# Depthwise convolution of an encoder layer: how its 31 taps are divided among the engines

## The chip, the cores and the metric

The kernel runs on one core of one Trainium2 chip. The metric is the device time of one execution in microseconds (us). The core has a matrix engine (TensorE, "PE" in the rows; "PEld" is its weight load), a vector engine (VectorE, DVE), a scalar engine (ScalarE, ACT), a general engine (GpSimd, POOL) and a queue engine (SyncE, SP) that issues most of the transfers. Each engine takes its instructions in order from a queue of its own; semaphores tie the queues together.

## The reference

One layer on 1024 tokens of width 1024, in float32. A first sub-layer projects the normalised input and splits the columns in two groups: a convolution module and an RWKV-7 recurrence in chunks; both go through one output projection. A second sub-layer chooses 128 of 16384 one-neuron experts for each token. The part that the change touches is the causal depthwise convolution over 31 taps and 512 channels:

```
u = p_conv[..., :CONV_WIDTH] * jax.nn.sigmoid(p_conv[..., CONV_WIDTH:])
u = lax.conv_general_dilated(u, conv_w[:, None, :], window_strides=(1,),
    padding=[(CONV_KSIZE - 1, 0)], feature_group_count=CONV_WIDTH) + conv_b
y_conv = silu(layer_norm(u, conv_ln_g, conv_ln_b))
```

Every channel has 31 weights of its own, so a tap is one multiplication by a weight per channel and one addition. Channels lie on the 128 partitions (four tiles `ct` of 128), tokens along the free dimension, in two halves of 512.

## The kernel before, in words

Two halves of the sequence, `h` = 0 and 1, are projected by `inproj(h)`: it normalises the tokens, transposes them to channels (`to_channels`, L210), splits them and the weights in two terms, and multiplies each weight tile in 24 matmuls (`proj`, L182). A projected tile leaves PSUM by two ScalarE copies and one VectorE operation (`shifted`, L325 to L329); `mixed` (L384) makes the operands of the recurrence from it, with two multiplications on GpSimd (L409, L421). `cond_some` (L248) reduces rows of the conditioning weights on VectorE in between. `glu` fills `ubuf`, the input of the convolution, and appends the generator `conv(h)` to the list `slow`.

The recurrence runs over 16 chunks: `solve(c)` and `pass_state(c)` are long chains of small matmuls on TensorE (L604, L635, L655, ...) with VectorE and ScalarE steps between them. After every few of their matmuls `fill()` is called: it advances the list `side` (`inproj(1)`, then the output projections `post`) by `RUN` = 4 steps whenever the credit allows, and with every fourth call (`SLOW` = 4) it advances `slow` by one `yield`. So one `yield` of `conv` is the unit in which the convolution is spread over the recurrence. `conv(0)` lies beside the start of the recurrence and `inproj(1)`. `conv(1)` begins when `inproj(1)` has written its last `u` and lies beside `post(0)`, the output projection of the first 256 tokens, which splits its weights with GpSimd (L170). What is left of `conv(1)` is drained at chunk 8 (L975).

`conv(h)` does for each of four channel tiles: one VectorE `tensor_scalar` (tap 0 with the bias, L453), 17 VectorE `scalar_tensor_tensor` (taps 1 to 17, L458, `a = u*w + a`, both `u` and `a` in SBUF), and for taps 18 to 30 a diagonal matrix made by ScalarE (L464, 128 x 128) and a float32 matmul of it with the window of `u` (L466, two matmul records each), summed in PSUM in `pt`. At the end `V.tensor_add(a, a, pt)` (L469) joins the two. Three VectorE taps and two matmul taps make one `yield`: 7 yields for a tile. After the four tiles the layer norm over channels follows (L472 to L484), then the swish (L488 to L491) and the store to `conv_d`.

The pages of the shared pool `pgp` (`NPAGE` = 35 pages of 128 x 512) hold `cacc` (L451), `ctap` (L462) and nearly every other temporary of `inproj`, `conv` and `post`. PSUM tiles `mm` are three (`NMM`); `pt` holds one of them for as long as a tile's taps last.

The order on each engine is not written out by hand: a scheduler of the framework takes, for each engine, the ready instruction that stands earliest in the program, by its own estimate of times, and fixes the order at compile time. On the chip the queues then run in that order, whatever the true durations are.

After the recurrence come the last `post`, the choice of experts (`choose`, `gate_matrix`) and the expert stage (L1156, L1190), which begins at about 1600 us and takes the rest.

Of the kernel before, what the change touches and what calls it, by code (L numbers as in the profile page):

```python
# [15 lines left out]
AF = mybir.ActivationFunctionType  # L16
# [9 lines left out]
KS = 31  # L26
# [53 lines left out]
def layer_kernel(ctx, tc, x, cols, c_row, cond_w, w_in, w2a2, g2, w_out, ln_rows, wq, keys, peer_u, peer_ut, peer_v, peer_vt, out):  # L80
    nc = tc.nc
    V, A, G, T = nc.vector, nc.scalar, nc.gpsimd, nc.tensor
# [10 lines left out]
    def col(n, i=None):  # L93
        a, b = COFF[n]
        return colt[:, a:b] if i is None else colt[:, a + i:a + i + 1]
# [50 lines left out]
    def mm(w=512):  # L146
        return psum.tile([128, 512], F32, tag="mm", name="mm")[:, :w]
# [4 lines left out]
    def page(name, dt=F32, w=512):  # L152
        return pgp.tile([128, max(w, 512)], dt, tag="pg", name=name)[:, :w]
# [117 lines left out]
    def inproj(h, ps, pg_):  # L271
# [60 lines left out]
        def glu():  # L332
            while conv_left:
                slow_step(1)
            for ct in range(4):
                if first and ct == 0:
                    pa, pg = first
                else:
                    pa = yield from tile_of(ct)
                    pg = yield from tile_of(4 + ct)  # L340
                s_ = tp("gsig")
                A.activation(s_, pg, AF.Sigmoid)
                A.activation(ubuf[:, ct, :KS - 1], utail[:, ct, :], AF.Copy)
                V.tensor_mul(ubuf[:, ct, KS - 1:], pa, s_)
                A.activation(utail[:, ct, :], ubuf[:, ct, HALF:], AF.Copy)
                if h == 1:
                    cond_some(range(32 + 4 * ct, 36 + 4 * ct))
            slow.append(conv(h))
            conv_left.append(h)
# [90 lines left out]


    slow, gates, gb, conv_left, psg, tail = [], [], [], [], [], []
    PE_TAPS = 13

    def conv(h):
        acc = []
        for ct in range(4):
            wk = lambda k: colt[:, COFF["conv_w"][0] + KS * ct + k:COFF["conv_w"][0] + KS * ct + k + 1]
            win = lambda k: ubuf[:, ct, k:k + HALF]

            a, pt = page("cacc"), mm()  # L451
            acc.append(a)
            V.tensor_scalar(a, win(0), wk(0), col("conv_b", ct), op0=OP.mult, op1=OP.add)  # L453
            i, j = 1, KS - PE_TAPS
            while i < KS - PE_TAPS or j < KS:
                for _ in range(3):
                    if i < KS - PE_TAPS:
                        V.scalar_tensor_tensor(a, win(i), wk(i), a, op0=OP.mult, op1=OP.add)  # L458
                        i += 1
                if j < KS:  # L460
                    n = min(2, KS - j)
                    dg = page("ctap").rearrange("p (k c) -> p k c", k=4)  # L462
                    for k in range(n):
                        A.activation(dg[:, k, :], ident, AF.Copy, scale=wk(j + k))  # L464
                    for k in range(n):
                        T.matmul(pt, dg[:, k, :], win(j + k), start=j + k == KS - PE_TAPS, stop=j + k == KS - 1)  # L466
                    j += n
                yield
            V.tensor_add(a, a, pt)  # L469
        pmn = mm()  # L470
        for ct in range(4):
            T.matmul(pmn, ones_m, acc[ct], start=ct == 0, stop=ct == 3)  # L472
        for ct in range(4):
            V.tensor_sub(acc[ct], acc[ct], pmn)
        yield
        pv = mm()
        for ct in range(4):
            s2 = page("s2")
            A.activation(s2, acc[ct], AF.Square)
            T.matmul(pv, ones_m, s2, start=ct == 0, stop=ct == 3)  # L480
        rs = page("crs")
        A.activation(rs, pv, AF.Sqrt, bias=eps_ln)
        V.reciprocal(rs, rs)
        yield  # L484
        for ct in range(4):
            y = acc[ct]
            V.tensor_mul(y, y, rs)
            A.activation(y, y, AF.Identity, bias=col("cln_b", ct), scale=col("cln_g", ct))  # L488
            sc_ = page("csig")
            A.activation(sc_, y, AF.Sigmoid)  # L490
            G.tensor_mul(y, y, sc_)  # L491
            ld(conv_d[h][ct], y)
            yield
        conv_left.remove(h)
# [643 lines left out]
    for g in range(32):  # L1138
# [4 lines left out]
        for e in range(4):  # L1143
# [7 lines left out]
            for bs in NBLK:  # L1151
                p = mg(NW)
                i = 0
# [99 lines left out]
```

## Time and profile before

| | us |
|---|---|
| median of 3 runs | 3366.39 (3362.37 to 3373.07) |
| the profiled execution | 3369.74 |
| its span, first to last instruction | 3367.7 |
| mean granted share of TensorE's clock in it | 0.936 |

The rows below come from that one profiled execution. In the rows an instruction stands as engine, line, operation, output and inputs by the program's names. "Busy" is the time in which an engine executes; the chain is the sequence of work that ended last, followed back from the end of the program, each step from what released it or from the instruction before it on its engine. The convolution lies in two stretches, from 215 to 330 us (`conv(0)`) and from 535 to 640 us with a remainder to 720 us (`conv(1)`).

### The profile page before, as it was taken

The page shows a single profiled execution, that of the slowest core. Times are in us where ns is not written, and L with a number is a line of the kernel's source. Part 1 is how long each engine was busy: PE and PEld are TensorE (multiplying, and loading weights), DVE is VectorE, ACT ScalarE, POOL GpSimd, SP SyncE. Part 2 cuts the span into 40 slices and gives each one's busy share as a digit, 9 for nine tenths or more (in the row PEclk, how much of TensorE's full clock was granted, in tenths as well). Part 3 has the DMA queues.
Part 4 walks back from the last instruction along what each step waited for, and adds up shares of the span by engine and source line. Part 5 has one row for each costly group of instructions (what it writes and reads, how often), then busy time and mean ns, then how long its engine had stood idle before and what let it go on. Part 6 is the DMA issues. An engine that isn't in the chain of part 4 may idle for free.

```text
span 3367.7 us, 54601 instructions
## 1 busy us (share of the span) xinstructions
PE 3039.8 (90%) x20400; PEld 2652.4 (79%) x20400; DVE 2523.1 (75%) x5590; ACT 1246.3 (37%) x2479; POOL 1734.8 (52%) x1328
## 2 busy tenths in 40 slices
PE   6969999999888665676999999999999999999996
PEld 5735766678777665675899999999999989998985
DVE  5398567657676697779777778777787877777788
ACT  5552543443545435654322222322222232222222
POOL 2400112234122154313877777787777768777772
PEclk9979999799889777787999999999999999999998
DMA  8875564467556757465999999898999989999994
GB/s 307 292 258 170 163 178 163 155 236 269 168 194 206 250 173 230 141 213 174 360 345 330 348 333 342 323 361 324 356 330 346 327 327 347 349 337 342 332 345 163
DMA packets 398393, 918.09 MB, mean 273 GB/s; under 512 B 77184, under 2 KB 210480, under 8 KB 376112
## 3 DMA queue, kind: packets, MB, share of 16 engines
q1 hardware_dynamic: 205296, 469.96, 39.8%
q0 software_dynamic: 110592, 402.70, 32.4%
q10 hardware_dynamic: 82240, 41.94, 4.4%
q8 instruction: 160, 2.62, 0.3%
q14 instruction: 105, 0.86, 0.1%
HBM read 786.55 MB, written 127.95 MB: 272 GB/s over the span
## 4 chain that ended last, share of the span: by engine, by line
PE 71%; DVE 14%; DMA 8%; ACT 3%; issue 2%; POOL 1%; SPq 0%; DVEq 0%; POOLq 0%; ACTq 0%
PE mg L1156 25%; PE md L1190 25%; PE mm L182 11%; DMA G_d<-stage 5%; PE mgate L958 3%; DVE cacc L458 2%; DVE cw L248 1%; PE bank L635 1%; DVE oa L940 1%; DVE ob L952 1%; PE bank L655 1%; DMA cw<-cond_w 1%; PE mm L828 1%; PE mm L466 1%; PE bank L604 1%
## 5 line engine op out<-in xcount | busy, mean ns | idle before, releaser
L1156 PE MATMUL mg<-h2h,uhi 128*128 128x320 f32 x2048 | 634.0, 310 | 0.0
L1156 PE MATMUL mg<-h2l,uhi 128*128 128x320 f32 x2048 | 633.8, 309 | 0.0
L1156 PE MATMUL mg<-h2h,ulo 128*128 128x320 f32 x2048 | 633.5, 309 | 0.0
L1190 PE MATMUL md<-vhi,ah 128*128 128x512 f32 x1280 | 492.7, 391 | 23.0 <-ACT vhi L1119 16.1
L1190 PE MATMUL md<-vhi,al 128*128 128x512 f32 x1280 | 498.2, 390 | 0.0
L1190 PE MATMUL md<-vlo,ah 128*128 128x512 f32 x1280 | 497.0, 390 | 0.0
L1093 DVE SCALAR_TENSOR_TENSOR gy<-grow,gz,gy 128x1024 f32<-128x1024 f32 x381 | 488.6, 1282 | 6.4 <-DMA grow<-peer_v,eid 2.7
L1086 DVE SCALAR_TENSOR_TENSOR grow<-grow,gh 128x1024 f32<-128x1024 f32 x384 | 458.9, 1213 | 34.8 <-DMA grow<-peer_u,eid 30.9
L1078 POOL DMA_INDIRECT grow<-peer_v,eid x384 | 361.0, 940 | 163.4 <-DVE gy L1093 85.0
L1078 POOL DMA_INDIRECT grow<-peer_u,eid x384 | 361.4, 941 | 159.6 <-issue 70.8
L1156 PEld LDWEIGHTS mg<-h2h,uhi 128*128 128x128 f32 x2048 | 385.8, 188 | 6.0
L1156 PEld LDWEIGHTS mg<-h2l,uhi 128*128 128x128 f32 x2048 | 385.8, 188 | 5.1
L1156 PEld LDWEIGHTS mg<-h2h,ulo 128*128 128x128 f32 x2048 | 385.6, 188 | 3.9
L1119 ACT ACTIVATE vhi<-vraw 128x1024 fp32r<-128x1024 f32 x128 | 135.6, 1062 | 635.4 <-PE md L1190 434.8
L1195 DVE TENSOR_TENSOR yacc<-md,yacc 128x512 f32<-128x512 f32 x310 | 210.6, 688 | 186.5 <-PE md L1190 180.7
L1121 POOL TENSOR_TENSOR vlo<-vraw,vhi 128x1024 fp32r<-128x1024 f32 x128 | 306.3, 2414 | 68.7 <-ACT vhi L1119 62.7
L958 PE MATMUL mgate<-oa,ob 128*128 128x128 f32 x1280 | 213.3, 321 | 141.2 <-ACT stage L959 97.3
L1121 POOL TENSOR_TENSOR ulo<-uraw,uhi 128x1024 fp32r<-128x1024 f32 x128 | 310.9, 2429 | 50.0 <-ACT uhi L1119 43.6
L958 PEld LDWEIGHTS mgate<-oa,ob 128*128 128x128 f32 x1280 | 190.8, 228 | 154.3 <-ACT stage L959 92.2
L1190 PEld LDWEIGHTS md<-vhi,ah 128*128 128x128 f32 x1280 | 240.7, 188 | 70.7 <-ACT vhi L1119 16.4
L1190 PEld LDWEIGHTS md<-vlo,ah 128*128 128x128 f32 x1280 | 240.3, 188 | 48.5
L1190 PEld LDWEIGHTS md<-vhi,al 128*128 128x128 f32 x1280 | 240.3, 188 | 44.0
(347 smaller groups left out, 5837.7 us busy)
## 6 DMA issues: line engine op xcount, KB each, us to landing
uraw<-peer_ut SPq DMA_DIRECT2D x128, 512.0 KB
vraw<-peer_vt SPq DMA_DIRECT2D x128, 512.0 KB
wsplit<-split_wq SPq DMA_DIRECT2D x48, 1024.0 KB
G_d<-stage ACTq DMA_DIRECT2D x20, 2048.0 KB
gmat<-G_d SPq DMA_DIRECT2D x32, 1280.0 KB
cw<-cond_w SPq DMA_DIRECT2D x48, 512.0 KB
wsplit<-split_w_out SPq DMA_DIRECT2D x24, 1024.0 KB
split_w_in<-wsplit SPq DMA_DIRECT2D x22, 1024.0 KB
```

Source lines behind the costliest of these rows:

```text
L182: T.matmul(pt, l[:, k, :], r[k], start=i == 0, stop=i == 3 * KD - 1)
L248: V.scalar_tensor_tensor(w, w, 1.0, silc, op0=OP.mult, op1=OP.mult, accum_out=mod[:, j:j + 1])
L458: V.scalar_tensor_tensor(a, win(i), wk(i), a, op0=OP.mult, op1=OP.add)
L958: T.matmul(pt[:, t, :], ob[:, t, :], oa[:, t, :], start=True, stop=True)
L1078: G.indirect_dma_start(out=r, out_offset=None, in_=peer_u if k < 128 else peer_v, in_offset=bass.IndirectOffsetOnAxis(ap=eid[:, k % 128:k ...
L1086: V.scalar_tensor_tensor(r, r, 1.0, ht, op0=OP.mult, op1=OP.mult, accum_out=z[:, i:i + 1])
L1093: V.scalar_tensor_tensor(y, r, z[:, i - 128:i - 127], y, op0=OP.mult, op1=OP.add)
L1119: A.activation(hi, raw, AF.Copy)
L1121: G.tensor_sub(lo, raw, hi.bitcast(F32))
L1156: T.matmul(p, l[:, k, :], r[k][:, bs], start=i == 0, stop=i == 3 * KD - 1)
L1190: T.matmul(p, l[:, ts], r[:, e % 2, :], start=e == 0 and q == 0, stop=e == 3 and q == 2)
L1195: V.tensor_add(ya, p, ya)
```

## The change

The taps 18 to 30 of TensorE are divided again. Taps 18 to 23 become six ScalarE products (`activation` with Copy and a scale per channel, 128 x 512): the first is written to a new page `cgps` (`b`), the other five to pages `cprod`, each of which GpSimd adds to `b`. Taps 24 to 30 stay on TensorE as diagonal products, seven in place of thirteen. At the end of a tile GpSimd adds `b` to `a`, and then VectorE adds `pt` as before. VectorE keeps the taps 0 to 17. One `yield` now holds four VectorE taps, one product with its addition, and two matmul taps: 5 yields for a tile in place of 7.

```
-    PE_TAPS = 13
+    PE_TAPS, POOL_TAPS = 7, 6
...
-            a, pt = page("cacc"), mm()
+            a, b, pt = page("cacc"), page("cgps"), mm()
...
-            i, j = 1, KS - PE_TAPS
-            while i < KS - PE_TAPS or j < KS:
-                for _ in range(3):
-                    if i < KS - PE_TAPS:
+            n_dve = KS - PE_TAPS - POOL_TAPS
+            A.activation(b, win(n_dve), AF.Copy, scale=wk(n_dve))
+            i, m, j = 1, n_dve + 1, KS - PE_TAPS
+            while i < n_dve or m < KS - PE_TAPS or j < KS:
+                for _ in range(4):
+                    if i < n_dve:
                         V.scalar_tensor_tensor(a, win(i), wk(i), a, op0=OP.mult, op1=OP.add)
                         i += 1
+                if m < KS - PE_TAPS:
+                    p_ = page("cprod")
+                    A.activation(p_, win(m), AF.Copy, scale=wk(m))
+                    G.tensor_add(b, b, p_)
+                    m += 1
                 if j < KS:
...
                 yield
+            G.tensor_add(a, a, b)
             V.tensor_add(a, a, pt)
```

## Rows read from the trace of the kernel before

**Rows 1.** The page: busy time by engine, and the chain by line.

```profile
PE 3039.8 (90%) x20400; PEld 2652.4 (79%) x20400; DVE 2523.1 (75%) x5590; ACT 1246.3 (37%) x2479; POOL 1734.8 (52%) x1328
...
PE mg L1156 25%; PE md L1190 25%; PE mm L182 11%; DMA G_d<-stage 5%; PE mgate L958 3%; DVE cacc L458 2%; DVE cw L248 1%; PE bank L635 1%; DVE oa L940 1%; DVE ob L952 1%; PE bank L655 1%; DMA cw<-cond_w 1%; PE mm L828 1%; PE mm L466 1%; PE bank L604 1%
```

**Rows 2.** Busy time of each engine by stretch; the header names the columns.

```profile
core 0: us, PE busy (x) PEld busy (x) DVE busy (x) ACT busy (x) POOL busy (x), PEclk, DMA share, GB/s
215.00:285.00 70.00, 61.17 (x176) 33.57 (x176) 69.81 (x122) 25.71 (x67) 4.75 (x3) 0.92 0.81 246
285.00:330.00 45.00, 41.22 (x277) 26.79 (x277) 40.55 (x101) 12.81 (x32) 1.50 (x1) 0.89 0.43 136
330.00:440.00 110.00, 109.91 (x1077) 79.79 (x1077) 60.46 (x110) 53.63 (x106) 13.67 (x11) 1.00 0.54 162
535.00:600.00 65.00, 60.74 (x408) 39.18 (x409) 56.89 (x75) 22.68 (x58) 16.23 (x8) 0.95 0.35 124
600.00:640.00 40.00, 37.45 (x368) 27.14 (x367) 30.17 (x59) 13.82 (x31) 9.74 (x5) 0.87 0.54 184
640.00:680.00 40.00, 37.25 (x384) 29.98 (x383) 25.35 (x70) 19.28 (x43) 5.61 (x5) 0.50 0.43 123
```

**Rows 3.** The chain by line within 190 to 330, 535 to 640, 640 to 700 us.

```profile
by line: DVE cacc L458 25.5%; DVE cw L248 21.4%; PE mm L182 6.1%; DVE nr L402 4.7%; DMA cw<-cond_w 4.6%; DMA bv_d<-sq 3.2%; DMA xt<-x 2.9%; PE mm L472 2.7%; DVE hlo L220 2.6%; PE bank L604 1.7%; DVE cum L392 1.6%; DVE sq L417 1.4%; PE mm L4
...
by line: DVE cacc L458 38.1%; issue 14.6%; PE mm L466 13.9%; PE mm L182 11.8%; DMA ycf<-rwkv_d 4.7%; POOL wsplit L170 2.2%; PE bank L635 1.7%; POOL xt L788 1.7%; PE bank L661 1.6%; POOL yclo L762 1.5%; DVE cacc L469 1.2%; DVE MT L658 1.0%; 
...
by line: PE mm L182 15.6%; PE mm L466 10.0%; DMA xt<-x 8.1%; PE mm L216 7.2%; PE bank L693 6.1%; PE mm L472 6.1%; PE bank L691 5.9%; PE bank L635 4.8%; PE bank L655 4.3%; PE bank L604 3.3%; DVE bnst L190 3.2%; PE bank L643 2.4%; PE bank L73
```

**Rows 4.** Single lines: ns least/median/most, first and last start in us.

```profile
L458 DVE SCALAR_TENSOR_TENSOR cacc<-u,colt,cacc x136: 628/747/2908, 218.1 to 634.0; 128x512 f32<-128x512 f32 x136
...
L466 PE MATMUL mm<-u,ctap x208: 590/592/1221, 217.4 to 691.4; 128*128 128x512 f32 x104
...
L464 ACT ACTIVATE ctap<-ident,colt x104: 384/390/414, 214.0 to 681.8; 128x128 f32<-128x128 f32 x104
...
L479 ACT ACTIVATE s<-cacc x8: 629/633/658, 326.4 to 698.9; 128x512 f32<-128x512 f32 x8
...
L491 POOL TENSOR_TENSOR cacc<-cacc,csig x8: 1265/1282/1735, 349.1 to 718.8; 128x512 f32<-128x512 f32 x8
```

**Rows 5.** Timeline, 215 to 264 us: start us, us, engine, line, names, count.

```profile
220.30 4.45 PE L466 MATMUL mm<-u,ctap 128*128 128x512 f32 x10
...
229.41 1.02 PE L419 MATMUL m<-sq,ones_h 128*128 128x512 f32 x2
...
248.29 1.44 POOL L409 TENSOR_TENSOR a<-a,nr 128x512 f32<-128x512 f32 x1 [22.68 <-DVE nr L404]
248.52 1.76 DVE L458 SCALAR_TENSOR_TENSOR cacc<-u,colt,cacc 128x512 f32<-128x512 f32 x1
...
259.29 1.40 DVE L458 SCALAR_TENSOR_TENSOR cacc<-u,colt,cacc 128x512 f32<-128x512 f32 x2
...
261.28 2.41 DVE L458 SCALAR_TENSOR_TENSOR cacc<-u,colt,cacc 128x512 f32<-128x512 f32 x2
261.49 1.66 POOL L421 TENSOR_TENSOR xm<-xm,W 128x512 f32<-128x512 f32 x1 [11.76 <-issue]
```

**Rows 6.** Groups by line, 190:330 (first two) and 535:640: busy us, mean ns.

```profile
L458 DVE SCALAR_TENSOR_TENSOR cacc<-u,colt,cacc 128x512 f32<-128x512 f32 x68 | 51.9, 789 | 0.1
L248 DVE SCALAR_TENSOR_TENSOR cw<-cw,silc 128x1024 f32<-128x1024 f32 x27 | 32.7, 1215 | 1.4 <-DMA cw<-cond_w 1.4
...
L458 DVE SCALAR_TENSOR_TENSOR cacc<-u,colt,cacc 128x512 f32<-128x512 f32 x68 | 62.3, 917 | 1.5
L170 POOL TENSOR_TENSOR wsplit<-wraw,wsplit 128x1024 fp32r<-128x1024 f32 x8 | 20.0, 2504 | 64.4 <-ACT wsplit L169 64.4
```

**Rows 7.** Line 466 alone, 285 to 330 us: PE busy and weight loads.

```profile
285.00:330.00 45.00, 11.43 (x26) 4.83 (x26) 0.89 0.43 136
```

**Rows 8.** Timeline, 676 to 700 us, of ScalarE and of VectorE.

```profile
679.82 1.85 ACT L464 ACTIVATE ctap<-ident,colt 128x128 f32<-128x128 f32 x6
...
692.05 0.69 DVE L469 TENSOR_TENSOR cacc<-cacc,mm 128x512 f32<-128x512 f32 x1 [10.36 <-PE mm L466]
```

## The prediction

> **What bounds the kernel now.** I read the page first. Half of the chain is the expert stage, lines 1156 and 1190 [rows 1], which the change does not touch. The line that the change thins out, 466, is about 1% of the chain; the vector taps of line 458, of which it keeps all, are 2% [rows 1]. So the question is what ends last in the two stretches where the convolution runs, not what is busiest over the span.
>
> The second view is busy time by stretch. From 215 to 285 us VectorE is busy for 69.81 of 70 us, TensorE for 61.17, GpSimd for 4.75; from 285 to 330 VectorE has 40.55 of 45 and TensorE 41.22; from 535 to 600 VectorE has 56.89 of 65 and TensorE 60.74 [rows 2]. Two engines are nearly full, so the table can't tell which is last. The chain does: from 190 to 330 us its first two lines are VectorE's taps (25.5%) and VectorE's reductions of line 248 (21.4%); line 466 stands nowhere in the list, whose last whole entry is 1.4%. From 535 to 640 us the taps of VectorE are 38.1%, which is 40 of 105 us, and line 466 is 13.9%, 14.6 us [rows 3]. Between the two, from 330 to 440 us, TensorE is busy for 109.91 of 110 us [rows 2], but no tap is in it. The reader is to see that VectorE bounds both stretches, with TensorE close behind, and that the change leaves VectorE its taps 0 to 17: 18 before, 18 after. "Divided in three" is a division of TensorE's thirteen.
>
> The third view is the timeline, for what a new GpSimd instruction does to VectorE. Two taps alone take 1.40 us; two taps with a GpSimd multiplication of 1.66 us beside them take 2.41. One tap has a median of 747 ns [rows 4]; with a GpSimd multiplication of 1.44 us beside it one takes 1.76 [rows 5]. Both times VectorE loses 1.0 us. The groups agree: in the second stretch, where line 170 runs on GpSimd for 20.0 us, the same 68 taps take 62.3 us, against 51.9 in the first [rows 6].
>
> **The change part by part.** *Additions on GpSimd.* A tile gets five additions of products and one of `b` to `a`: 6, so 24 in each `conv(h)`, 48 in all. The nearest row for one is line 491, the same shape, median 1.28 us [rows 4]; they are 31 us for each `conv`, and GpSimd has that room in both stretches [rows 2]. The price is VectorE's: 1.0 us for each that meets a tap [rows 5]. It can be nothing, where the addition meets an idle VectorE, and 1.28, where VectorE stands still for all of it; I take 1.0, since the two measured cases are of this very instruction on VectorE and of GpSimd instructions of this shape. How many meet: VectorE is busy for 110.4 of 115 us from 215 to 330, 96%, and line 248, its other large load there, 32.7 us, also reads two tiles of SBUF [rows 2, 6]. That gives 24 x 1.0 x 0.96 = 23 us for `conv(0)`. For `conv(1)` I count three tiles, 18 additions, because the last tile's taps on TensorE come only after ScalarE has made their matrices at 680 us, when VectorE idles for 10.36 us before line 469 [rows 8]; there I read a lack of free pages, and the additions of the last tile, which need pages too, would wait with them. VectorE is busy for 87.1 of 105 us, 83%: 18 x 1.0 x 0.83 = 15 us. Together 38 us of VectorE, all on its queue, in stretches where the chain runs through that queue.
>
> The Trainium skill, "SBUF — State Buffer", section "Who interferes with whom", has a rule that speaks against this change: a VectorE instruction with two SBUF inputs and a GpSimd instruction that reads SBUF exclude each other for the whole instruction. The two cases above agree in kind; by the whole instruction the 42 additions would cost 42 x 1.28, before the shares some 54 us in place of 42, and the sum would be about 10 us higher.
>
> *Matmuls off TensorE.* 6 taps x 8 tiles = 48 taps of two records each. Ten records in a row take 4.45 us, or 0.43 us apart when the last one's 0.59 is taken off [rows 4, 5] (4.45 - 0.59, over 9), so 48 x 2 x 0.43 = 41 us leave TensorE. What of it is on the chain: 14.6 us of line 466 from 535 to 640, 6.0 us from 640 to 700 (10.0% of 60), and under 1.4% of 140 us, 2 us, in the first stretch [rows 3]: some 22 us, of which 6/13 go, 10 us. To that I add the taps from 285 to 330 us, 11.43 us [rows 7], of which 6/13 are 5 us: what TensorE has done by then of the projections shortens the stretch after 330, where it is full. So -15; the bounds are -10 and -41. I stay near the lower one because while VectorE is the later engine a freer TensorE finds nothing ready.
>
> *ScalarE.* 48 diagonal matrices of 390 ns go, 48 products come; the nearest row is line 479, 128 x 512 from SBUF, 633 ns [rows 4]: +11.7 us, under a ScalarE that is busy for 25.71 of 70 us [rows 2]. I count nothing; without that cover it would be the 11.7.
>
> *Waits.* `V.tensor_add(a, a, pt)` now waits for GpSimd's last addition, which waits for the tile's last tap: 1.28 us or more, 8 times, with the next tile's taps and line 248 queued behind it on VectorE. The scheduler can put those in front, so I take 0 of a bound of 10 us. On GpSimd the multiplications of lines 409 and 421, in the first stretch, and the subtraction of line 170, in the second, now queue behind additions, one of which waits for VectorE; a queue fixed at compile time by times that a blocked VectorE does not keep makes them late. TensorE's order shows how freely the scheduler mixes: taps of `conv(0)` stand at 220 us, ahead of line 419 of the earlier `inproj(0)` at 229 [rows 5]. Bound 0 to 10 us, taken 0. `yield`s fall from 7 to 5 for a tile, so the convolution is asked for earlier beside the recurrence; total VectorE work to its end is the same, so I count 0, and no sign is excluded. Five `cprod` and one `cgps` page come for a tile and three `ctap` pages go, which can only lengthen the wait for pages.
>
> The sum on the profiled execution: 3369.7 + 23 + 15 - 15 = 3392.7 us. That execution is 3.3 us over the median of the runs, so on medians 3366.4 + 23 = 3389.4; I say 3389.
>
> **The rivals.** *TensorE was the bound after all (faster).* It is busy for 98.2 of 105 us in the second stretch and for 109.91 of 110 from 330 to 440 [rows 2]. If the additions fall where VectorE waits or works from one tile, and TensorE uses the freed time for projections ahead of the full stretch, -15 to -41 is left: 3325 to 3351, say 3340. It decides from the point where fewer than about 15 of the 42 additions meet a busy VectorE. Against it stands a VectorE with 0.2 us of idle time in 70.
>
> *The two balance.* Half of the additions meet a tap, 19 us, against 15 to 20 of TensorE: 3356 to 3376, say 3366. For it speaks that from 600 to 640 us VectorE has 9.8 us free [rows 2].
>
> *A late queue or a slower clock on top of the forecast.* From 640 to 680 us TensorE runs at a granted share of 0.50, its lower level of 1.2 GHz, and is busy for 37.25 us [rows 2], which at 2.4 GHz would be about 18.6. A TensorE with 41 us less to do idles more beside VectorE; one more stretch like this costs some 18 us, and so do the two queue waits above together at their bounds: 3407. The Trainium skill, "TensorE: Matmul & The Clock Gate", section "What's actually happening", says that "the default state is throttled, and activity releases the throttle", by which removing matmuls has this price; the rows show only that the clock was 0.87 from 600 to 640 us and 0.50 after it, not what it fell for.
>
> **How the numbers follow.** Forecast 0.55, balance 0.18, TensorE as the bound 0.18, late queue or clock 0.09. The predicted time is the forecast's, 3389. Its own range runs from 3377 (-15 becomes -27) to 3412 (all 42 additions at the 1.28 bound, no relief beyond 10 us: 3366 + 54 - 10 = 3410). For 8 in 10 I take in the balance and the start of the faster rival, and above it most of the late queue: 3350 to 3420, which leaves out about 0.16 below and 0.03 above. A difference of 0.3%, 10 us, is about what a measurement of this kernel can tell from no change. Slower by more: 0.55 + 0.09 = 0.64; within: 0.18; faster by more: 0.18.
>
> **What would show it.** Right: line 458 with a mean well over 0.79 us in the first stretch (about 1.1 with some 20 additions in it), taps that end after GpSimd's additions, the first chunk's operands and the end of `conv(0)` some 20 us later, and TensorE with more idle time before 330 us. Wrong: taps still at 0.75 us beside additions (the price); additions in gaps of VectorE (the count); the stretch from 330 us on shortened by as much as the first grew (the relief); a mean clock lower than 0.936 of the span with VectorE unchanged (the clock).

## The result

The changed kernel takes 3392.53 us in the median (3390.59 to 3395.66), the kernel before 3365.66 beside it (3362.37 to 3373.07). The ratio is 1.0076, with a 95% interval of 1.006 to 1.0092: slower by 27 us. The profiled execution took 3390.64 us, span 3388.8, granted clock 0.928.

The page after, busy time by engine and the chain by line (compare [rows 1]):

```profile
PE 3024.6 (89%) x20304; PEld 2651.0 (78%) x20304; DVE 2583.2 (76%) x5590; ACT 1261.0 (37%) x2479; POOL 1820.5 (54%) x1376
...
PE mg L1165 25%; PE md L1199 25%; PE mm L182 9%; DMA G_d<-stage 4%; DVE cacc L461 3%; PE mgate L967 2%; DVE cw L248 2%; DVE oa L949 1%; DVE ob L961 1%; DMA cw<-cond_w 1%; PE bank L644 1%; DVE oh L907 1%; PE bank L664 1%; DVE vi L845 1%; DVE
```

VectorE is busy for 60 us more, GpSimd for 86, TensorE for 15 less. In the chain VectorE's taps, now line 461, rise from 2% to 3%; the projections of line 182 fall from 11% to 9%, and the store of `stage` (`G_d<-stage`) from 5% to 4%. The waits for that store begin more than 500 us behind the end of the convolution, and they matter below.

Busy time by stretch (compare [rows 2]; columns as there):

```profile
core 0: us, PE busy (x) PEld busy (x) DVE busy (x) ACT busy (x) POOL busy (x), PEclk, DMA share, GB/s
215.00:285.00 70.00, 38.97 (x92) 19.63 (x90) 70.00 (x83) 32.51 (x69) 32.79 (x20) 0.79 0.53 159
285.00:330.00 45.00, 21.07 (x88) 13.95 (x88) 44.55 (x91) 2.43 (x7) 5.42 (x4) 0.59 0.65 193
330.00:440.00 110.00, 108.25 (x1078) 78.79 (x1078) 63.70 (x131) 48.01 (x100) 15.71 (x13) 0.98 0.45 143
535.00:600.00 65.00, 60.34 (x527) 42.00 (x525) 43.05 (x51) 24.82 (x54) 34.23 (x20) 0.92 0.49 163
600.00:640.00 40.00, 29.30 (x193) 20.54 (x193) 39.75 (x44) 19.39 (x39) 29.14 (x17) 0.83 0.25 83
```

VectorE has no idle time from 215 to 285 us, and 0.45 of 45 us from 285 to 330, where it had 4.45 before. TensorE is busy for 60 us in these two stretches, against 102 before. Some 19 to 21 us of that difference are taps that are gone: 54 of their records stand in the two stretches, where there were 104. The rest is projections (66 records in place of 119) and matmuls of the recurrence's first chunks that have not been reached yet. The granted clock fell with it, from 0.92 to 0.79 and from 0.89 to 0.59. From 330 us on TensorE is full as before, so that what came late stays late: the last `u` of the second half (line 344) is written at 555 us, 32 us later than before.

The chain by line within 190 to 330 and 535 to 640 us (compare [rows 3]):

```profile
by line: DVE cacc L461 30.7%; DVE cw L248 23.7%; DMA cw<-cond_w 9.7%; DVE nr L402 4.7%; DVE hlo L220 4.2%; DVE cacc L454 2.7%; DVE a L410 2.4%; DMA bv_d<-sq 1.9%; DVE nr L413 1.6%; DVE cum L392 1.6%; DVE sq L407 1.6%; PE m L419 1.5%; DVE sq
...
by line: DVE cacc L461 55.7%; PE mm L182 7.2%; DMA ycf<-rwkv_d 6.3%; POOL wsplit L170 4.6%; DMA split_w_out<-wsplit 4.2%; DVE cacc L454 4.1%; issue 2.4%; ACT wsplit L169 2.0%; PE bank L613 1.9%; SPq L157 1.2%; DVE cacc L478 1.1%; SPq L601 1
```

VectorE's taps carry 30.7% and 55.7%, where they carried 25.5% and 38.1%; TensorE's taps are in neither list, as far as the lists are shown (down to 1.5% and 1.1%). The groups by line (busy us, mean ns | idle before), first from 190 to 345 us, then from 555 to 700 us, since `conv(1)` begins later (compare [rows 6]):

```profile
L461 DVE SCALAR_TENSOR_TENSOR cacc<-u,colt,cacc 128x512 f32<-128x512 f32 x68 | 57.6, 876 | 0.0
L248 DVE SCALAR_TENSOR_TENSOR cw<-cw,silc 128x1024 f32<-128x1024 f32 x27 | 37.0, 1373 | 0.8 <-DMA cw<-cond_w 0.8
L466 POOL TENSOR_TENSOR cgps<-cgps,cprod 128x512 f32<-128x512 f32 x20 | 32.0, 1607 | 14.9 <-ACT cprod L465 14.0
L454 DVE TENSOR_SCALAR cacc<-u,colt 128x512 f32<-128x512 f32 x4 | 4.0, 1010 | 0.0
...
L461 DVE SCALAR_TENSOR_TENSOR cacc<-u,colt,cacc 128x512 f32<-128x512 f32 x68 | 79.7, 1202 | 0.8
```

A tap has a mean of 876 ns in the first stretch (789 before) and of 1202 in the second (917). How it comes about is in the timeline from 242 to 252 us, VectorE's rows and one of GpSimd's (start, us, engine, line, names, count):

```profile
243.16 0.46 DVE L406 TENSOR_SCALAR sq<-a,colt 128x512 f32<-128x512 f32 x1
243.54 0.74 DVE L461 SCALAR_TENSOR_TENSOR cacc<-u,colt,cacc 128x512 f32<-128x512 f32 x1
243.84 7.82 POOL L466 TENSOR_TENSOR cgps<-cgps,cprod 128x512 f32<-128x512 f32 x5 [10.30 <-ACT cprod L465]
244.21 1.49 DVE L401 TENSOR_SCALAR nr<-nr 128x512 f32<-128x512 f32 x1
245.62 1.49 DVE L454 TENSOR_SCALAR cacc<-u,colt 128x512 f32<-128x512 f32 x1
247.03 1.76 DVE L461 SCALAR_TENSOR_TENSOR cacc<-u,colt,cacc 128x512 f32<-128x512 f32 x1
248.72 1.22 DVE L250 TENSOR_TENSOR mod<-mod,colt 128x4 f32<-128x4 f32 x1
249.86 0.68 DVE L393 TENSOR_TENSOR sig<-cum,sig 128x512 f32<-128x512 f32 x1
250.46 2.29 DVE L248 SCALAR_TENSOR_TENSOR cw<-cw,silc 128x1024 f32<-128x1024 f32 x1
```

Five additions run on GpSimd for 7.82 us, from 243.84 to 251.66. Beside them a tap takes 1.76 us in place of 0.74, line 248 takes 2.29 in place of 1.21, and even line 250, which touches 128 x 4 numbers, takes 1.22. Line 393 gets through at its usual 0.68: it begins 0.02 us before the fifth addition, and that addition takes 1.79 us. Line 250 begins 0.39 us after the fourth addition and ends 0.02 us after it. In these two cases the instruction that began later waited for the other one. (The row above merges the five additions; their single times stand in the trace.)

### The profile page after: what moved, and what is told of

Its sections match the earlier page's. It is cut to its first block, busy times and chain, and to the rows that moved or that the text cites. A ratio compares the mean times of both kernels' runs of the same rounds, so it can differ in the third digit from the quotient of the medians.

```text
span 3388.8 us, 54489 instructions
## 1 busy us (share of the span) xinstructions
PE 3024.6 (89%) x20304; PEld 2651.0 (78%) x20304; DVE 2583.2 (76%) x5590; ACT 1261.0 (37%) x2479; POOL 1820.5 (54%) x1376
## 4 chain that ended last, share of the span: by engine, by line
PE 68%; DVE 19%; DMA 7%; ACT 3%; issue 2%; POOL 1%; SPq 0%; ACTq 0%; DVEq 0%; POOLq 0%
PE mg L1165 25%; PE md L1199 25%; PE mm L182 9%; DMA G_d<-stage 4%; DVE cacc L461 3%; PE mgate L967 2%; DVE cw L248 2%; DVE oa L949 1%; DVE ob L961 1%; DMA cw<-cond_w 1%; PE bank L644 1%; DVE oh L907 1%; PE bank L664 1%; DVE vi L845 1%; DVE s L846 1%
```

## The experiments

Four theories are told apart. Theory 1: the additions hold VectorE up (in the first four runs it also held that fewer `yield`s give time back). Theory 2: it is the order of the queues and their waits. Theory 3: GpSimd's load as such is at fault, whatever it reads. Theory 4 came up after the first runs and speaks of an end order: some 25 us are given back in the last stretch before the experts, by the order in which the scheduler happens to put the instructions there. All ratios are against runs of the kernel before that were taken beside each group of experiments, with medians of 3367.5 to 3369.2 us; their 95% interval stands behind each. A ratio can differ from the quotient of the medians by up to 0.25%.

**The number of yields, alone.** The kernel before with 5 `yield`s for a tile, and the kernel after with 7:

```
a1_pace (from before)
-                for _ in range(3):
+                for _ in range(4):
...
-                    n = min(2, KS - j)
+                    n = min(3, KS - j)

a2_slow_pace (from after)
-                for _ in range(4):
+                for _ in range(3):
...
-                    n = min(2, KS - j)
+                    n = min(1, KS - j)
```

> The kernel before, with its 13 matmul taps and 18 vector taps, but four vector taps and three matmul taps in one yield, so that a tile takes 5 yields in place of 7. No GpSimd addition. In the changed kernel the lag behind the kernel before is about 42 us near 700 us and 14 us when the expert stage begins. Theory 1 (the additions cost VectorE time, and the shorter convolution lets the jobs behind it in the list of slow jobs start earlier, which gives some 25 us back later): faster than before by 10 to 30 us, 3336 to 3356. Theory 2 (what was given back is another order of the queues or chance, and 5 yields do nothing by themselves): within 10 us of 3366.

> The changed kernel with 7 yields for a tile: three vector taps, one product with its addition and one matmul tap in each. All 48 additions on GpSimd stay. Theory 1: what 5 yields gave back is gone, 3402 to 3422. Theory 2: as the changed kernel, 3383 to 3402.

Measured: a1 3366.83 us, ratio 0.9993 (0.998 to 1.0006); a2 3387.18 us, 1.0044 (1.0026 to 1.0062). The changed kernel with its seven yields back is no slower than with five; it is 5 us faster by the medians and some 11 by the ratios. That fewer yields give time back has fallen. That they cost nothing isn't shown: a1 takes the time of the kernel before, but with another order in the last stretch, and ahead of that stretch it is 17 us behind (the table below).

**The additions, taken away and alone.** In a3 the five additions of products to `b` are left out (taps 19 to 23 are missing from the sum; their products are still made). In a4 the kernel before gets six additions for a tile that nobody reads:

```
a3_no_adds (from after)
-                    G.tensor_add(b, b, p_)

a4_adds_alone (from before)
-            a, pt = page("cacc"), mm()
+            a, b, pt = page("cacc"), page("cgps"), mm()
+            q = 0
...
+                if q < 6:
+                    G.tensor_add(b, mask0, w2a2_t)
+                    q += 1
```

> The changed kernel without the 40 additions of products on GpSimd (taps 19 to 23 are left out of the sum); the products on ScalarE, the addition of b to a, the 5 yields and the 7 matmul taps stay. Theory 1: VectorE gets back about 1 us for each addition that met a busy VectorE; mean of the vector taps from 190 to 345 us back from 876 ns to about 790; 3392 - 30 to 45 = 3347 to 3362. Theory 2 (order and waits, not the additions beside VectorE): 3382 to 3400.

> The kernel before with six more additions on GpSimd for each tile, of two constant tiles in SBUF into a page that nobody reads: 48 in all, no wait for a product, 13 matmul taps, 7 yields. Theory 1: the price of the additions by themselves, without relief for TensorE and without the new pace: vector taps slowed as in the changed kernel and a lag of 30 to 45 us, 3396 to 3411, more than the change itself. Theory 2: 3360 to 3376.

Measured: a3 3342.61 us, 0.9925 (0.9903 to 0.9948); a4 3411.73 us, 1.0117 (1.0092 to 1.0143). Forty additions less are worth 50 us, 48 more cost 43. The groups from 190 to 345 us, of a3 (first) and of a4:

```profile
L461 DVE SCALAR_TENSOR_TENSOR cacc<-u,colt,cacc 128x512 f32<-128x512 f32 x68 | 53.5, 814 | 0.0
L248 DVE SCALAR_TENSOR_TENSOR cw<-cw,silc 128x1024 f32<-128x1024 f32 x27 | 32.6, 1211 | 0.0
L454 DVE TENSOR_SCALAR cacc<-u,colt 128x512 f32<-128x512 f32 x4 | 2.1, 534 | 0.0
```

```profile
L459 DVE SCALAR_TENSOR_TENSOR cacc<-u,colt,cacc 128x512 f32<-128x512 f32 x68 | 59.3, 893 | 0.1
L462 POOL TENSOR_TENSOR cgps<-mask,w2a_t 128x512 f32<-128x512 f32 x24 | 39.9, 1663 | 8.1 <-PE mm L470 6.6
L248 DVE SCALAR_TENSOR_TENSOR cw<-cw,silc 128x1024 f32<-128x1024 f32 x27 | 38.0, 1414 | 0.0
```

Without the additions all three VectorE lines are back near the values of before: 814, 1211 and, for the first tap, 534 ns against 1010. With additions that no one waits for they are held up again, 893 and 1414. No data ties a4's additions to VectorE's work, so it is not a wait. Theory 1 holds, with a3 4 us below the time that was expected by it and a4 just past the upper end of its range.

**What it is in an addition that holds VectorE up.** In b2 a memset of the same size stands in place of each addition (taps 19 to 23 are missing again). In b1 VectorE's taps are summed in PSUM instead: they begin on `pt` when the seven matmul taps have ended, and ScalarE's first product takes the bias.

```
b2_memset (from after)
-                    G.tensor_add(b, b, p_)
+                    G.memset(page("cz"), 0.0)

b1_psum_taps (from after)
-            V.tensor_scalar(a, win(0), wk(0), col("conv_b", ct), op0=OP.mult, op1=OP.add)
...
-            A.activation(b, win(n_dve), AF.Copy, scale=wk(n_dve))
+            A.activation(b, win(n_dve), AF.Identity, bias=col("conv_b", ct), scale=wk(n_dve))
...
-                        V.scalar_tensor_tensor(a, win(i), wk(i), a, op0=OP.mult, op1=OP.add)
...
-                    n = min(2, KS - j)
+                    n = min(4, KS - j)
...
+                else:
+                    for _ in range(6):
+                        if i < n_dve:
+                            V.scalar_tensor_tensor(pt, win(i), wk(i), pt, op0=OP.mult, op1=OP.add)
...
-            G.tensor_add(a, a, b)
-            V.tensor_add(a, a, pt)
+            V.tensor_add(a, b, pt)
```

> The changed kernel with a memset of a page on GpSimd in place of each of the 40 additions of products (taps 19 to 23 are left out of the sum): GpSimd's instructions in the same places, 128 x 512, but they read nothing from SBUF. Theory 1 (reading is what counts): no tap slowed, as the kernel without additions, 3333 to 3355. Theory 3: between that one and the changed kernel, 3360 or more.

> The changed kernel's division of the taps (18, 6, 7), but VectorE adds its taps in PSUM, in the bank where the seven matmul taps have been summed, so that each of its taps reads one tile from SBUF and one from PSUM; the bias goes into ScalarE's first product, and the tile ends with one VectorE addition of b and PSUM. The 40 additions on GpSimd stay. Theory 1 (a GpSimd addition that reads SBUF holds up a VectorE instruction that reads two tiles from SBUF): taps at 0.75 to 0.80 us beside additions; line 248 and the others of the first stretch, which still read two tiles from SBUF, are held up as before, so some 30 of the 50 us that the kernel without additions gained: 3345 to 3372. Theory 3 (it is GpSimd's load or the order of the queues as such, whatever VectorE reads): as the changed kernel, 3383 to 3402.

Measured: b2 3345.57 us, 0.9914 (0.9883 to 0.9944), as fast as a3. The groups of b2 from 190 to 345 us:

```profile
L461 DVE SCALAR_TENSOR_TENSOR cacc<-u,colt,cacc 128x512 f32<-128x512 f32 x68 | 52.6, 801 | 0.0
L466 POOL MEMSET cz<- 128x512 f32 x20 | 10.6, 538 | 23.8 <-PE mm L474 9.3 <-ACT cprod L465 7.0 <-ACT lw L356 6.7
```

The taps of b2 have a mean of 801 ns. By their start and end times in the trace 15 of all 136 run beside a memset and no other work of GpSimd, and these take 734 to 752 ns; the slow ones stand beside GpSimd's other instructions, which read. A GpSimd that only writes does VectorE no harm here. That speaks against theory 3, though a memset is only a third as long as an addition.

b1 took 3428.69 us, 1.016 (1.0123 to 1.0197): slower than all others and outside the ranges of both theories. Its taps, all of them (ns least, median, most), and what VectorE waited for in front of them (us, times):

```profile
L469 DVE SCALAR_TENSOR_TENSOR mm<-u,colt,mm x144: 675/749/757, 226.7 to 711.5; 128x512 f32<-128x512 f32 x144
...
  PE mm L464: 42.6, 5
```

All 144 taps lie between 675 and 757 ns; the same tap with both inputs in SBUF went up to 2870 ns in the changed kernel. By itself this shows less than it seems to. The 40 additions of products run on GpSimd as in the changed kernel (the eight of `b` to `a` are gone), but most of them meet no tap: only 4 of the 144 taps run beside one of them, and 29 beside any GpSimd instruction that reads, at 743 to 757 ns. What makes b1 slow is the new wait: VectorE stands still 42.6 us, five times, until the matmul taps have ended. The point is settled by the versions below, where taps of both kinds run beside additions in the same execution.

The Trainium skill, "SBUF — State Buffer", section "Who interferes with whom", states both halves: a VectorE instruction with two SBUF inputs contends with a GpSimd instruction that reads SBUF, and not with one that only writes it. The 1.76 us of a tap beside additions in the changed kernel and the 734 to 752 ns beside memsets in b2 agree. The page also says that a `tensor_scalar`, with one input, can contend in its two-port modes; line 454 was held up (1010 against 534 ns), but no run here shows in which mode it was.

**Versions without b1's wait.** In c3 VectorE's taps 0 to 6 go to SBUF and 7 to 17 to PSUM, once the matmul taps are done, with four matmul taps in a yield in place of two. b4 and c4 are b1 and c3 with ten GpSimd taps and 14 on VectorE.

```
c3_half_psum (from after)
-                    if i < n_dve:
-                        V.scalar_tensor_tensor(a, win(i), wk(i), a, op0=OP.mult, op1=OP.add)
+                    if i < n_dve and (i < 7 or j == KS):
+                        t_ = a if i < 7 else pt
+                        V.scalar_tensor_tensor(t_, win(i), wk(i), t_, op0=OP.mult, op1=OP.add)
...
-                    n = min(2, KS - j)
+                    n = min(4, KS - j)

b4_psum_14_10_7 (from b1), c4_half_psum_14 (from c3)
-    PE_TAPS, POOL_TAPS = 7, 6
+    PE_TAPS, POOL_TAPS = 7, 10
...
-                for _ in range(1):
+                for _ in range(2):
```

The last two lines, two products in a yield, are c4's alone.

> The changed kernel, but VectorE's taps 7 to 17 are added up in PSUM, on top of the seven matmul taps, and only taps 0 to 6 in SBUF, so that VectorE has work of its own until the matmul taps are there; the bank is queued at the end in the order of the kernel before. With all taps in PSUM no tap was held up by an addition, but VectorE stood idle for 42.6 us for line 464. Theory 1: 11 of 18 taps free of GpSimd, the idle time mostly gone, half of the price saved: lag of 10 to 25 us near 700 us, 3376 to 3396 with that end. Theory 3 (no gain from PSUM): as the changed kernel or slower, with its 25 us at the end missing: 3405 or more.

> As the kernel with VectorE's taps in PSUM, but 14 taps on VectorE, 10 as ScalarE products that GpSimd adds up and 7 on TensorE. Theory 1: 32 taps of 0.75 us less on VectorE, 32 more additions on GpSimd that meet only the instructions with two tiles from SBUF: 0 to 20 us faster than the kernel with 18 taps in PSUM. Theory 3: slower than it by 20 us or more.

> As the run above with 14 taps on VectorE (0 to 6 in SBUF, 7 to 13 in PSUM), 10 as products on ScalarE that GpSimd adds up, 7 on TensorE. Theory 1: 32 vector taps of 0.75 us less, 24 us, against 32 more additions that meet the taps in SBUF, line 248 and the others of two tiles: 0 to 20 us under the run above, apart from the order at the end, which is another one here: 3355 to 3396.

Measured: c3 3377.7 us, 1.003 (1.0016 to 1.0045); b4 3391.39 us, 1.0069 (1.0047 to 1.009); c4 3384.47 us, 1.0052 (1.0034 to 1.007). c3's taps by form (ns least, median, most), in PSUM and in SBUF:

```profile
L462 DVE SCALAR_TENSOR_TENSOR mm<-u,colt,mm x88: 667/743/756, 235.6 to 654.2; 128x512 f32<-128x512 f32 x88
L462 DVE SCALAR_TENSOR_TENSOR cacc<-u,colt,cacc x48: 723/762/2802, 222.6 to 639.5; 128x512 f32<-128x512 f32 x48
```

And of c4:

```profile
L462 DVE SCALAR_TENSOR_TENSOR mm<-u,colt,mm x56: 673/744/757, 239.4 to 639.2; 128x512 f32<-128x512 f32 x56
L462 DVE SCALAR_TENSOR_TENSOR cacc<-u,colt,cacc x48: 736/1636/1829, 222.3 to 630.7; 128x512 f32<-128x512 f32 x48
```

In c3 17 of the 88 PSUM taps run beside an addition of products, at 709 to 749 ns, and 18 of the 48 SBUF taps, with a mean of 1651 ns. In c4 it is 29 of 56 PSUM taps, at 720 to 757 ns, and 39 of 48 SBUF taps, with a mean of 1523. The engine, the operation, the size and the additions are the same, and only the place of one input differs: a tap with one input in SBUF and one in PSUM is not held up. With that theory 3 has fallen. VectorE's wait for the matmul taps is gone as well, but for 0.3 us in c4.

c3 keeps the changed kernel's division of the taps and costs 10 us in place of 27, though its end order, that of the kernel before, gives next to nothing back (below). Four more GpSimd taps in place of VectorE's make b4 37 us faster than b1 (0 to 20 were expected, and the end order differs) and c4 7 us slower than c3, where 0 to 20 us less were expected; ahead of the last stretch c4 is 23 us behind c3. No version that does the whole computation beats the kernel before.

**The matmuls, taken away alone.** b3 is the kernel before with seven matmul taps and nothing for the other six (taps 18 to 23 are missing from the sum):

```
b3_relief (from before)
-    PE_TAPS = 13
+    PE_TAPS, OUT = 7, 6
...
-            while i < KS - PE_TAPS or j < KS:
+            for _ in range(7):
...
-                    if i < KS - PE_TAPS:
+                    if i < KS - PE_TAPS - OUT:
```

> The kernel before with taps 18 to 23 left out: seven matmul taps in place of thirteen, 18 vector taps, 7 yields, no product on ScalarE, nothing new on GpSimd. It is the relief of TensorE by itself. My sum had 15 us of it with bounds of 10 and 41; the kernel without additions came out 27 us under the kernel before with the products on ScalarE and 5 yields. Relief as that run shows it: 3335 to 3350, of which some 25 would be the other order of the last stretch before the expert stage, where the lag should jump between 1250 and 1530 us; relief as in my sum: 3350 to 3358; none: 3360 or more.

Measured: 3350.28 us, 0.9922 (0.9895 to 0.995), 18 us less by the medians and 26 by the ratio. It looks as if the -15 of the sum were confirmed. Where the 18 us lie says otherwise. I took the start of the same instruction in each trace and subtracted its start before: the first copy of expert scores (line 831 of before, at 720 us), the 23rd (at 1221), the first matmul of the experts (line 1156, at 1535; ahead of the prediction that start was put at about 1600), and the end of the span. The order is the sequence of ScalarE's gate, query and score copies (lines 959, 823 and 831) from 1221 to 1535 us; equal letters are equal sequences. (The norm copies of line 208 stand elsewhere among them in after and b3 than in the other four of order B.)

| kernel | order | 720 us | 1221 us | 1535 us | end |
|---|---|---|---|---|---|
| after | B | +25 | +36 | +14 | +21 |
| a1 | B | +4 | +17 | -6 | -1 |
| a2 | B | +29 | +34 | +15 | +20 |
| a3 | B | -17 | -21 | -41 | -35 |
| b3 | B | -16 | -2 | -21 | -17 |
| b4 | B | +33 | +37 | +16 | +20 |
| c3 | A, as before | +19 | +11 | +8 | +8 |
| c1 | C | -3 | -4 | -2 | -2 |
| c2 | C | +25 | +44 | +41 | +43 |
| a4 | D | +43 | +43 | +42 | +45 |
| b1 | E | +83 | +77 | +73 | +67 |
| b2 | E | -14 | +2 | -7 | -12 |
| c4 | F | +27 | +34 | +17 | +17 |

(The profiled executions lie up to 12 us off their medians: a3 8 below, b2 12 above. Single entries are good to about 10 us.) Two things are to be seen. b3 is 16 us ahead at 720 us and 2 us ahead at 1221: what a freer TensorE gains is mostly gone again before the last stretch. And every kernel of order B, whatever was done to its convolution, gains 19 to 23 us between 1221 and 1535 us; those of orders A, C and D gain none to 3, those of order E 4 and 9, and c4 with order F gains 17. a1 is the plainest case: it has the division of the taps of the kernel before and order B, and it gains 23.

**The end order, by itself.** c1 and c2 change nothing in the convolution. Each shifts by a small edit behind it what the scheduler meets first:

```
c1_before_turn (from before)
-    side.append(post(S - PB, cpage))
+    side.append(post(S - PB, cpage)); fills[0] += 1

c2_after_turn (from after)
-    side.append(post(S - PB, cpage))
+    side.append(post(S - PB, cpage)); slow_step(2)
```

> The kernel before with the count of fills moved on by one before the last loop (line 1007), which changes no computation and no order ahead of the last output projection; it only turns the order in which the last gate matrices and projections are queued. The kernel before waits in that stretch, from 1355 to 1490 us, 39 us for the stores of line 961; the changed kernel and four of the others, which have one other order there, wait 10 to 14 us and lose some 25 us of their lag. Theory 4 (the 25 us that the changed kernel gave back are this order and have nothing to do with the taps): the lag to the kernel before is 0 up to 1220 us and then a gain of 10 to 27 us, 3340 to 3358. Rival (the end of the recurrence and the taps set it): 3362 to 3372.

> The changed kernel with two more steps of the slow list ahead of the last loop, after which the last gate matrices and projections are queued in the same order on ScalarE as in the run above. Theory 4: against the run above, which has the same order at the end, the change costs what its lag shows ahead of that stretch, 30 to 42 us; so 3372 to 3398. Rival: the difference between the two is that of the two kernels without the turn, 20 to 27 us.

Measured: c1 3367.75 us, 1.0007 (0.9993 to 1.0021); c2 3407.42 us, 1.0114 (1.0093 to 1.0136). c1 missed the time expected by theory 4 and lies where the rival had it, because it did not get the cheaper order that it was to try; so c2 lies above its range too. But both got the same order, C, and the test is in their difference: c2 less c1, 40 us, is the price of the change at equal order, where theory 4 expected 30 to 42 and the rival 20 to 27. What goes with the order is a wait of ScalarE for a store: `stage` is written again (line 959, after 968) when its transfer to `G_d` is done. The waits (us, times, longest) in the last stretch, of before (1355 to 1490 us), after (1387 to 1500), c1 (1350 to 1490) and c2 (1400 to 1535), one fence each:

```profile
ACT stage L959 <- DMA G_d<-stage: 39.4, 5, 11.8
```

```profile
ACT stage L968 <- DMA G_d<-stage: 10.0, 3, 5.1
```

```profile
ACT stage L959 <- DMA G_d<-stage: 30.2, 5, 10.4
```

```profile
ACT stage L968 <- DMA G_d<-stage: 25.3, 5, 10.6
```

39.4 us before, 10.0 after, 30.2 and 25.3 in the two kernels of order C: the changed kernel lost its wait for the store, and c2, with the same convolution, has it again. From the 23rd score copy to the first matmul of the experts ScalarE waits 35 to 49 us for this store in the six kernels of order B and 57 to 71 in the five of A, C and D, and the stretch takes 291 to 295 us in B and 310 to 315 in A, C and D. Theory 4 holds as far as this: the gain goes with the order, not with the convolution. That the shorter wait for the store is its whole cause is not shown by a run of its own, and why the scheduler picks B for one kernel and A or C for another is open.

## Why the prediction came true

3389 us were forecast, 3392.5 were measured, and the direction was right. The steps are less right than the number.

- *VectorE bounds both stretches.* Right: its taps rise in the chain, TensorE's leave it, and VectorE has 0.45 us free in 115.
- *The price of an addition, 1.0 us of VectorE.* Right. 68 taps x (876 - 789) and 68 x (1202 - 917) are 5.9 + 19.4 = 25 us. Line 248 adds 27 x (1373 - 1215) = 4.3, and lines 454, 220 and 410 another 11, summed over the trace up to 1240 us: 41 us in five lines, where 38 were forecast.
- *How it shows.* Half wrong. I expected a mean near 1.1 us for a tap in the first stretch and it was 0.88: other VectorE instructions took the rest of the delay, some with one input or with only a few numbers. GpSimd's own additions, which I had at 1.28 us, have a mean of 1.61.
- *Six additions of the last tile that cost nothing.* Wrong. I read a lack of pages from VectorE's idle 10.36 us [rows 8]. After the change VectorE is busy for 39.75 of 40 us from 600 to 640, and the last tile is joined at 662 us, not 692. The additions cost 43 us (a4, 48 of them) to 50 us (a3, 40 of them), so this term was some 5 to 12 us short.
- *The wait of `V.tensor_add(a, a, pt)`.* Right: taken at nothing, and the trace has one wait of 1.2 us there. GpSimd waits instead for the taps, 56.7 us in eight waits, and nobody misses it.
- *ScalarE and its products at nothing.* Right: its busy time grew by 14.7 us (the 48 swaps were put at 11.7), and a3, which still makes the products, is no slower than b3, which does not.
- *Matmuls off TensorE, -15 us.* Not confirmed. b3, which has nothing but the relief, shows 16 us at 720 us and 2 of them at 1221, and its shorter time is the end order. But a3, which has the relief with the products and five yields, is 21 us ahead at 1221 (some 13 if its profiled execution, 8 us below its median, is allowed for). By these two the relief is worth between 2 and some 20 us ahead of the last stretch, and no run narrows it down.
- *Yields at nothing.* Not shown. a1 is 17 us behind at 1221 us, and its time comes out even only by order B; a2 is 5 us faster than the changed kernel with the same order. The bound without a sign was earned.
- *The step that was mis-sized.* For the convolution the sum was +23; the lag at 1221 us is +36, and at equal order the runs show +40. Of the 17 us that are missing, 5 to 12 are the additions, of which the last tile's six were counted at nothing. The other 5 to 12 must lie in what is left, the relief and the yields, and how they are shared is open.
- *What the sum left out.* An order of the last stretch that is worth about 20 us. The change costs +40 at equal order. The order gave back 13: 3407.4 - 3392.5 is 15, of which 2 are the difference between the medians of the kernel before that were taken beside the two. Together they are the +27 that was measured. The forecast was near by luck: a loss forecast 17 us too small, and a gift of 13 to 20 us that no row of the convolution could show. (A slip beside this: the forecast's own range is said to end at 3412, and its sum gives 3410.)

Of the rivals, TensorE as the bound and the balance did not come. The slower clock came in part: 0.59 from 285 to 330 us, but in a stretch in which TensorE waits for VectorE; the row of 330 to 440 us is full again at 0.98. From 640 to 680 us, the stretch that this rival went by, the clock is higher than before, at 0.91 in place of 0.50. The price of the 0.59 was not measured by itself; it may be part of what makes the +18 us at `conv(0)`'s last VectorE tap (337.0 us in place of 319.0) +32 by the last `u`. In b3 the first two stretches have 0.79 and 0.80, and it is 16 us ahead at 720 us all the same.

## What to carry to other kernels

An addition that is handed to GpSimd is not free for VectorE: look at what VectorE reads in that stretch, and if both operands are in SBUF, count about 1 us of VectorE for each 128 x 512 addition. Moving one VectorE operand to PSUM takes the cost away, but only if that PSUM tile is ready when VectorE wants it. And where a compiler fixes the queues' order, compare two variants at an equal order in the stages that the edit doesn't touch; here the same edit measured as +27 us or as +40.

## What the runs showed of the hardware

- Beside GpSimd additions VectorE instructions with one SBUF input were held up as well: two `tensor_scalar` of 128 x 512 took 1.49 us each, in place of 0.53 (line 454) and 0.42 (line 401, which has only constants beside its input). A 128 x 4 `tensor_tensor` took 1.22 in place of 0.16.
- The lengthening is mutual: GpSimd's 128 x 512 addition of a product has a median of 1.27 us in b1, where most of them meet no tap, and of 1.60 in the changed kernel, as the trace records them.
- VectorE taps with both inputs in SBUF kept 734 to 752 ns beside GpSimd memsets of the same tile (b2, 15 taps), and taps with one input in PSUM kept 709 to 757 ns beside GpSimd additions (c3 and c4, 46 taps).
- Between 285 and 330 us TensorE's granted clock is 0.59 in the changed kernel and 0.89 in the one before, while its work fell from 277 records to 88 and its busy time from 41.2 to 21.1 us of 45.
